# The modulation's matrix handed over transposed, its column sums taken by multiply-and-sum instructions on VectorE

## The chip, the cores and the metric

The kernel runs on one core of a Trainium2 chip. The metric is the time of one execution on the device, in microseconds (us): the median of three runs where several are shown. The engines that matter are TensorE (PE in the rows; PEld is its weight load), VectorE (DVE), ScalarE (ACT), GpSimd (POOL) and SyncE (SP, which issues nearly all DMAs). All data are 32-bit floats.

## The reference

Two transformer blocks are computed one after the other on 256 tokens of width 2048. The first is modulated by a condition vector `c`: six vectors of 2048 numbers (shift, scale and gate for the mixer, shift, scale and gate for the FFN) come from one large matrix-vector product, and everything in the block waits for some of them.

```python
c_act = jax.nn.silu(c)                       # 1 x 2048
mod = c_act @ w_ada[l] + b_ada[l]            # w_ada: 2048 x 12288
sh1, sc1, gt1, sh2, sc2, gt2 = jnp.split(mod, 6, axis=-1)
h = modulate(rms_norm(x, g_mix[l]), sh1, sc1)    # h * (1 + sc1) + sh1
z = h @ w_in[l]                              # projections, attentions, merge
x = x + gt1[:, None, :] * (merged @ w_out[l])
h = modulate(rms_norm(x, g_ffn[l]), sh2, sc2)
a = causal_dwconv(h @ w_gate[l], conv_w[l], conv_b[l])
x = x + gt2[:, None, :] * ((silu(a) * (h @ w_up[l])) @ w_down[l])
```

The second block has no modulation. `w_ada` is 2048 x 12288 numbers, 100.7 MB of the 581 MB that the kernel reads from HBM.

## The kernel before

Activations lie transposed: 128 features on the partitions, 256 tokens along a row. Weights stream through `rawp`, a pool of 6 buffers of 128 x 1024 numbers (10 at first, with `rawx`), each filled by one DMA from SP's queue. What is loaded, and in which order, is the list `items`: ("w", ...) is a piece of a weight matrix, ("ada", a, ...) a piece of `w_ada`, ("call", f) a function run at that point. `pump_loads` keeps up to `state["raws"]` items in flight beyond those already consumed.

A weight piece is consumed by `split`: ScalarE writes a rounded copy `wh` (line 296), VectorE the rest `wl = raw - wh` (line 303), and TensorE then does three products for each 128 x 128 tile (`mm_f`, lines 393 to 401, and `mm_t`, lines 412 to 414). `run` splits three pieces ahead of the one that TensorE multiplies (`AHEAD`). Everything is in program order on each engine; side work (attention, norms) is written as generators that `tick` moves on after a set amount of TensorE work.

**The modulation before.** `mod` is 128 x 96: column c holds features 128c to 128c+127 of the product. The 96 columns are taken in 28 groups (`ADA`): 12 groups of 2 or 3 columns for the first shift and scale, 16 groups of 4 columns for the rest. A piece of group `a` holds a few of the 16 row blocks k of `w_ada`, and `split` (lines 306 to 335) multiplies row block k, with the rows on the partitions, by the 128 numbers `cact[:, k]` and adds it into an accumulator `adaacc`. Two accumulators are filled side by side: VectorE does its share with one multiply-and-add each (line 330; the first with line 325), ScalarE scales the others (line 327) and GpSimd adds them (line 328). `ada_finish` lets GpSimd add both (line 366), and TensorE sums over the partitions by a product with a column of ones (line 370), from which VectorE writes `mod` (line 348). The first two groups, on which the first projection waits, are done in a hurry: of 16 row blocks VectorE takes ten and TensorE six (lines 321 and 355).

**Order around the change.** At the start SP loads `vec` (small vectors, `c` among them), `xT` and the first pieces. ScalarE computes `silu(c)` into `cact` (line 586, 128 x 16), then the squares of x (line 594); VectorE adds them up (lines 597, 598), TensorE sums over the partitions (line 601), `first_norm` turns the sums into `rb` (lines 607 to 613), `h_scale` multiplies x by it (line 626), `h_prep` applies the modulation (lines 635 to 648), and the first projection starts (line 399). The projections run in six stages of 2, 2, 3, 3, 3 and 3 row blocks (`KG`); during stage j the two groups that stage j + 1 needs are loaded and summed, mixed with the pieces of `w_in`. This lasts until about 415 us. The other 16 groups are spread over the gates, `w_o_sb`, `w_o_dsa`, `w_out` (until about 880 us) and the first FFN half, until 1040 us. `open_ffn` (line 1136), called before the first product with `w_out`, closes the pool `ab` of the first part and opens that of the FFN.

Of the kernel before, what the change touches and what calls it, by code (L numbers as in the profile page):

```python
# [28 lines left out]
FIRST_OWN = [k for k in range(16) if k % 8 not in (1, 4, 6)]  # L29
# [8 lines left out]
FW = (3, 3, 10)  # L38
# [16 lines left out]
VEC = [("c", 16), ("b_ada", 96), ("g_mix", 16), ("g_ffn", 16), ("g_final", 16), ("attn_norm", 16),  # L55
# [68 lines left out]
def kernel(ctx: ExitStack, tc: tile.TileContext, t):  # L124
# [30 lines left out]
    cact = const.tile([128, 16], F32, name="cact")  # L155
# [87 lines left out]
    def ada_items(a):  # L243
        return [("ada", a, k, n) for k, n in pieces(NK, 128 * ADA[a][1])]
# [7 lines left out]
    def load(idx):  # L252
# [11 lines left out]
        w = sum(g.width for g in it[1]) if it[0] == "w" else 128 * ADA[it[1]][1]  # L264
        r = raw_of[idx] = r[:, :n * w].rearrange("p (k w) -> p k w", w=w)
        if it[0] == "w":
            off = 0
            for width, src, c0, rmap in join([p for g in it[1] for p in g.parts]):
                nc.sync.dma_start(out=r[:, :, off:off + width], in_=rows(src, rmap(k0), n, c0, width))
                off += width  # L270
        else:
            nc.sync.dma_start(out=r, in_=rows(t["w_ada"], k0, n, 128 * ADA[it[1]][0], w))
# [9 lines left out]

    ada_acc = {}

    def split(idx, g, ks, off, stage):
# [20 lines left out]
        a = it[1]  # L306
        first = a in (0, NKG)
        if stage == 0 and k0 == 0:
            ada_acc[a] = P.get("ft", ab).tile([128, 2, 512], F32, name="adaacc", tag="adaacc", bufs=2)
            if first:  # L310
                ada_ps[a] = psm()
        for k in ks:
            side = k not in FIRST_OWN if first else k % 3 == 1 if a < 2 * NKG else k % 2 == 1
            if side != (stage == 0):
                continue
            own = FIRST_OWN.index(k) if first and not side else k // 2
            acc = ada_acc[a][:, own % 2 if first else int(side), :128 * ADA[a][1]]
            x, cs = r[:, k - it[2], :], cact[:, k:k + 1]
            if side and first:
                for j in range(ADA[a][1]):  # L320
                    nc.tensor.matmul(ada_ps[a][:, j:j + 1], x[:, 128 * j:128 * (j + 1)], cs,
                                     start=(k == 1 and j == 0), stop=False)
            elif own < (2 if first else 1):
                eng = nc.gpsimd if side else nc.vector
                eng.tensor_scalar(out=acc, in0=x, scalar1=cs, scalar2=None, op0=OP.mult)
            elif side:
                nc.scalar.activation(out=x, in_=x, func=AF.Copy, scale=cs)  # L327
                nc.gpsimd.tensor_tensor(out=acc, in0=x, in1=acc, op=OP.add)  # L328
            else:
                nc.vector.scalar_tensor_tensor(out=acc, in0=x, scalar=cs, in1=acc, op0=OP.mult, op1=OP.add)  # L330
        if stage == 1 and ks[-1] == NK - 1:
            if first:
                ada_first(a)
            else:
                fins.append(start(ada_finish(a)))

    ada_ps = {}
    ada_done = set()
    fins = []

    def need_ada(a, b):
        while not set(range(a, b)) <= ada_done:
            tick()

    def ada_put(a, ps, step):
        c, n = ADA[a]
        b = VOFF["b_ada"][0] + c
        nc.vector.tensor_add(out=mod[:, c:c + n], in0=ps[:, 0:step * n:step], in1=vec[:, b:b + n])
        ada_done.update(range(c, c + n))

    def ada_first(a):
        acc, ps, w = ada_acc.pop(a), ada_ps[a], 128 * ADA[a][1]
        nc.vector.tensor_add(out=acc[:, 0, :w], in0=acc[:, 0, :w], in1=acc[:, 1, :w])
        for j in range(ADA[a][1]):
            nc.tensor.matmul(ps[:, j:j + 1], acc[:, 0, 128 * j:128 * (j + 1)], ones[:, 0:1], start=False,
                             stop=(j == ADA[a][1] - 1))
        if a == 0:
            h_scale(0)
            ada_put(NKG, ada_ps[NKG], 1)
            ada_put(0, ps, 1)  # L360
# [1428 lines left out]
```

## Time and profile before

| | before |
|---|---|
| median of 3 runs | 2815.79 us (2815.03 to 2815.88) |
| the profiled execution, its own time | 2818.41 us |
| its span in the trace | 2816.6 us |
| TensorE busy | 2734.5 us (97%), 18364 instructions |
| VectorE busy | 2007.7 us (71%), 2804 instructions |
| ScalarE busy | 1424.9 us (51%), 2124 instructions |
| GpSimd busy | 841.1 us (30%), 710 instructions |
| DMA | 590.45 MB, mean 210 GB/s |

The page of the profile cuts the span into 40 slices and gives the busy share of each engine in tenths. TensorE reads 7899999899999999 for the first 16 slices and 9 in all that follow; VectorE 7999997979888986 first and 5 to 7 afterwards; GpSimd 3867752545754531 first and 0 to 3 afterwards. So the first 1030 us, in which the modulation runs, are the stretch where engines other than TensorE are full; after that TensorE is alone. A TensorE that reads as busy is not always multiplying at its peak, since the ends of its pipelined instructions are modelled: the idle time before an instruction, and what ended it, say more than the busy share.

### The profile page before, as it was taken

Reading aid. Unit: us, or ns where it says so; the run is one execution under the profiler, and the core shown is the slowest. Engines: PE = TensorE matmul, PEld = TensorE weight load, DVE = VectorE, ACT = ScalarE, POOL = GpSimd, SP = SyncE. Lnnn points to the kernel's source line nnn. Section 1 sums busy time; section 2 is a strip of 40 time slices with the busy share of each in tenths; the row PEclk is TensorE's granted clock in tenths of the full one; section 3 lists DMA queues with packets and bytes.
Section 4 is the critical chain, followed back from the end, with each engine's and each line's share of the span. In section 5 each row is a group of like instructions: output and inputs, shape, how many; then the busy total and the mean of one; then the engine's idle time right before and its main releaser. Section 6 shows DMA issues by size and latency. Waiting matters only on the chain.

```text
span 2816.6 us, 47791 instructions
## 1 busy us (share of the span) xinstructions
PE 2734.5 (97%) x18364; PEld 2496.7 (89%) x18364; DVE 2007.7 (71%) x2804; ACT 1424.9 (51%) x2124; POOL 841.1 (30%) x710
## 2 busy tenths in 40 slices
PE   7899999899999999999999999999999999999999
PEld 7788887788988999989999888989998888888888
DVE  7999997979888986655666765676776665556654
ACT  5555564555556554434454544555554544344443
POOL 3867752545754531000110310211222220012210
PEclk9999999999999999999999999999999999999999
DMA  9777777878887876566666575544566565566654
GB/s 316 250 249 256 241 219 203 268 242 280 291 276 233 287 260 183 184 188 186 180 180 191 183 229 172 163 123 144 186 188 187 180 189 193 187 187 187 187 195 142
DMA packets 334944, 590.45 MB, mean 210 GB/s; under 512 B 21234, under 2 KB 85594, under 8 KB 334716
## 3 DMA queue, kind: packets, MB, share of 16 engines
q1 hardware_dynamic: 331236, 583.61, 65.7%
q10 hardware_dynamic: 3480, 3.79, 0.7%
q8 instruction: 144, 2.36, 0.3%
q14 instruction: 84, 0.69, 0.1%
HBM read 581.49 MB, written 5.78 MB: 209 GB/s over the span
## 4 chain that ended last, share of the span: by engine, by line
PE 76%; DVE 10%; DMA 5%; issue 4%; POOL 3%; ACT 2%; SPq 0%; DVEq 0%; ACTq 0%; POOLq 0%
PE pg L397 25%; PE pg L396 13%; PE pg L399 9%; PE pg L400 9%; PE pg L401 9%; DVE wl L303 4%; DVE adaacc L330 3%; PE pg L393 2%; DMA raw<-in_w_in 2%; PE pm L728 1%; PE pg L412 1%; ACT wh L296 1%; PE pg L414 1%; PE pg L413 1%; DMA raw<-in_w_out 1%
## 5 line engine op out<-in xcount | busy, mean ns | idle before, releaser
L303 DVE TENSOR_TENSOR wl<-raw,wh 128x1024 fp32r<-128x1024 f32 (+1 forms) x921 | 1192.1, 1306 | 658.3 <-ACT wh L296 656.1
L296 ACT ACTIVATE wh<-raw 128x1024 fp32r<-128x1024 f32 (+2 forms) x922 | 934.2, 1026 | 883.2 <-PE pg L397 497.6
L397 PE MATMUL pg<-ring,wh 128*128 128x512 f32 x3384 | 1203.9, 396 | 0.0
L396 PE MATMUL pg<-ring,wl 128*128 128x256 f32 x3384 | 957.9, 283 | 7.6 <-DVE wl L303 7.6
L399 PE MATMUL pg<-ring,wh 128*128 128x256 f32 (+1 forms) x2828 | 813.7, 288 | 9.8 <-DVE ring L1093 3.6
L401 PE MATMUL pg<-ring,wl 128*128 128x256 f32 (+1 forms) x2828 | 799.9, 283 | 13.9 <-DVE wl L303 13.8
L400 PE MATMUL pg<-ring,wh 128*128 128x256 f32 (+1 forms) x2828 | 803.7, 284 | 0.0
L397 PEld LDWEIGHTS pg<-ring,wh 128*128 128x128 f32 x3384 | 638.2, 189 | 141.4
L396 PEld LDWEIGHTS pg<-ring,wl 128*128 128x128 f32 x3384 | 638.4, 189 | 23.6 <-DVE wl L303 9.5
L401 PEld LDWEIGHTS pg<-ring,wl 128*128 128x128 f32 x2828 | 541.4, 191 | 17.8 <-DVE wl L303 17.8
L399 PEld LDWEIGHTS pg<-ring,wh 128*128 128x128 f32 x2828 | 538.2, 190 | 19.7 <-issue 7.6
L400 PEld LDWEIGHTS pg<-ring,wh 128*128 128x128 f32 x2828 | 539.5, 191 | 3.6 <-issue 2.2
L531 POOL TENSOR_TENSOR ring<-gy,ring 128x256 fp32r<-128x256 f32 x88 | 107.1, 1230 | 661.9 <-ACT ring L529 661.9
L328 POOL TENSOR_TENSOR adaacc<-raw,adaacc 128x512 f32<-128x512 f32 (+2 forms) x152 | 230.6, 1517 | 247.4 <-ACT raw L327 197.4
L330 DVE SCALAR_TENSOR_TENSOR adaacc<-raw,cact,adaacc 128x512 f32<-128x512 f32 (+2 forms) x228 | 234.2, 1031 | 3.6 <-DMA raw<-in_w_ada 2.0
L1268 POOL TENSOR_TENSOR gy<-ga,rb 128x256 f32<-128x256 f32 x44 | 53.6, 1228 | 331.1 <-ACT ga L203 331.1
L516 POOL TENSOR_TENSOR ring<-pt,ring 128x256 f32<-128x256 f32 x95 | 109.7, 1167 | 50.5 <-ACT pt L515 50.3
L327 ACT ACTIVATE raw<-raw,cact 128x512 f32<-128x512 f32 (+2 forms) x152 | 103.1, 681 | 23.3 <-DMA raw<-in_w_ada 16.9
L1163 POOL TENSOR_TENSOR ssq<-ssq,sq 128x256 f32<-128x256 f32 x60 | 63.8, 1075 | 145.3 <-ACT sq L1161 144.0
L1406 POOL TENSOR_TENSOR hm<-hm,hsq 128x512 f32<-128x512 f32 (+1 forms) x15 | 18.4, 1224 | 286.3 <-ACT hsq L203 286.3
L393 PE MATMUL pg<-ring,wh 128*128 128x512 f32 x200 | 81.9, 410 | 7.0 <-DVE ring L1169 3.6
L412 PE MATMUL pg<-wh,ring 128*128 128x512 f32 (+3 forms) x236 | 84.2, 357 | 0.0
(300 smaller groups left out, 2665.1 us busy)
## 6 DMA issues: line engine op xcount, KB each, us to landing
raw<-in_w_in SPq DMA_DIRECT2D x240, 512.0 KB, 4.6
raw<-in_w_gate SPq DMA_DIRECT2D x176, 512.0 KB, 4.2
raw<-in_w_up SPq DMA_DIRECT2D x176, 512.0 KB, 4.4
raw<-in_w_down SPq DMA_DIRECT2D x176, 512.0 KB, 4.2
raw<-in_w_ada SPq DMA_DIRECT2D x144, 512.0 KB, 5.4
raw<-in_w_out SPq DMA_DIRECT2D x64, 512.0 KB, 4.6
raw<-in_w_ada SPq DMA_DIRECT2D x64, 384.0 KB, 4.1
raw<-in_w_o_sb SPq DMA_DIRECT2D x16, 512.0 KB, 5.1
```

What stands on the lines that cost most here:

```text
L296: nc.scalar.activation(out=hi, in_=src, func=AF.Copy)
L303: nc.vector.tensor_sub(out=lo, in0=src, in1=hi.bitcast(F32))
L328: nc.gpsimd.tensor_tensor(out=acc, in0=x, in1=acc, op=OP.add)
L330: nc.vector.scalar_tensor_tensor(out=acc, in0=x, scalar=cs, in1=acc, op0=OP.mult, op1=OP.add)
L393: nc.tensor.matmul(g.ps[f], hi[:, fs], both, start=True, stop=False)
L396: nc.tensor.matmul(ps, lo[:, fs], xh, start=False, stop=False)
L397: nc.tensor.matmul(g.ps[f], hi[:, fs], both, start=False, stop=stop)
L399: nc.tensor.matmul(ps, hi[:, fs], xh, start=start, stop=False)
L400: nc.tensor.matmul(ps, hi[:, fs], xl, start=False, stop=False)
L401: nc.tensor.matmul(ps, lo[:, fs], xh, start=False, stop=stop)
L412: nc.tensor.matmul(ps, xh[:, bs], hi, start=start, stop=False)
L516: nc.gpsimd.tensor_tensor(out=y, in0=x, in1=y, op=OP.add)
```

## The change

`w_ada` is handed over transposed (`w_adaT`, 12288 x 2048, prepared outside the kernel as the other inputs are), and an item is now one half of a column block: 128 outputs on the partitions, 1024 of the 2048 inputs along the row. One VectorE instruction multiplies the piece by the same half of `silu(c)`, which lies in every partition (`cb`, 128 x 2048), and sums along the row into `mod[:, c]`. The first half starts from `b_ada`, the second from what the first left. ScalarE, GpSimd and TensorE no longer take part.

To have `silu(c)` in every partition, `c` is loaded as one row, TensorE multiplies it by a row of ones (four products of 128 x 512), and ScalarE writes the silu of each into `cb`. One row of it goes to HBM (`cdram`), since the pool with `cb` is closed by `open_ffn`; there a second `cb` is opened and filled from `cdram` by a DMA from ScalarE's queue.

```diff
     def ada_items(a):
-        return [("ada", a, k, n) for k, n in pieces(NK, 128 * ADA[a][1])]
+        return [("ada", a, i, 1) for i in range(2 * ADA[a][1])]
...
+        if it[0] == "ada":
+            raw_of[idx] = r
+            c, half = ADA[it[1]][0] + it[2] // 2, it[2] % 2
+            nc.sync.dma_start(out=r, in_=t["w_adaT"][128 * c:128 * c + 128, RAW * half:RAW * half + RAW])
+            return
...
-            if side and first:
-                for j in range(ADA[a][1]):
-                    nc.tensor.matmul(ada_ps[a][:, j:j + 1], x[:, 128 * j:128 * (j + 1)], cs,
-                                     start=(k == 1 and j == 0), stop=False)
-            elif own < (2 if first else 1):
-                eng = nc.gpsimd if side else nc.vector
-                eng.tensor_scalar(out=acc, in0=x, scalar1=cs, scalar2=None, op0=OP.mult)
-            elif side:
-                nc.scalar.activation(out=x, in_=x, func=AF.Copy, scale=cs)
-                nc.gpsimd.tensor_tensor(out=acc, in0=x, in1=acc, op=OP.add)
-            else:
-                nc.vector.scalar_tensor_tensor(out=acc, in0=x, scalar=cs, in1=acc, op0=OP.mult, op1=OP.add)
...
+        if stage == 0:
+            return
+
+        c, half = ADA[it[1]][0] + it[2] // 2, it[2] % 2
+        below = mod[:, c:c + 1] if half else V["b_ada"][:, c:c + 1]
+        nc.vector.tensor_tensor_reduce(out=r, in0=r, in1=P["cb"][:, RAW * half:RAW * half + RAW], scale=1.0,
+                                       scalar=below, op0=OP.mult, op1=OP.add, accum_out=mod[:, c:c + 1])
+        if half:
+            ada_done.add(c)
...
-    def ada_finish(a):
-        acc, w = ada_acc.pop(a), 128 * ADA[a][1]
-        s = acc[:, 1, :w]
-        yield
-        nc.gpsimd.tensor_tensor(out=s, in0=acc[:, 0, :w], in1=s, op=OP.add)
-        yield from wait(FW[a // NKG if a < 2 * NKG else 2])
-        ps = psm()
-        for j in range(ADA[a][1]):
-            nc.tensor.matmul(ps[:, j:j + 1], s[:, 128 * j:128 * (j + 1)], ones[:, 0:1], start=True, stop=True)
-        ada_put(a, ps, 1)
...
+    P["cb"] = ab.tile([128, D], F32, name="cb")
+    nc.sync.dma_start(out=P["cb"][0:1, :], in_=t["c"])
...
-    lut(out=cact, in_=V["c"], func=AF.Silu)
+    for u in range(4):
+        ps = psm()
+        nc.tensor.matmul(ps, ones[0:1, :], P["cb"][0:1, 512 * u:512 * u + 512], start=True, stop=True)
+        lut(out=P["cb"][:, 512 * u:512 * u + 512], in_=ps, func=AF.Silu)
+    cdram = dram.tile([1, D], F32, name="cdram")
+    nc.scalar.dma_start(out=cdram, in_=P["cb"][0:1, :])
...
-    a0, a1 = ada_items(NKG), ada_items(0)
+    a0 = ada_items(NKG) + ada_items(0)
     items.extend(a0[:2])
     call_item(first_norm)
-    items.extend(a0[2:] + a1)
+    items.extend(a0[2:-2])
+    call_item(lambda: h_scale(0))
+    items.extend(a0[-2:])
     call_item(first_h)
...
+            if first:
+                P["cb"] = P["ft"].tile([128, D], F32, name="cb", bufs=1)
+                nc.scalar.dma_start(out=P["cb"], in_=bass.AP(tensor=cdram.tensor, offset=cdram.offset,
+                                                             ap=[[0, 128], [1, D]]))
```

The programs of both kernels show where this puts the instructions. First ScalarE from the start of the program to `first_norm`; `mm` and `r` are the norm's scratch tiles. Before:

```order
L203 ACT_TABLE_LOAD
L203 ACTIVATE cact<-vec 128x16
L594 ACTIVATE ring<-ring 128x1024 x4
L607 ACTIVATE mm<-pm,epsc 128x256
L197 ACT_TABLE_LOAD
```

Now:

```order
L200 ACT_TABLE_LOAD
L200 ACTIVATE cb<-pm 128x512 x4
L538 DMA cdram<-cb 1x2048
L546 ACTIVATE ring<-ring 128x1024 x4
L559 ACTIVATE mm<-pm,epsc 128x256
L194 ACT_TABLE_LOAD
```

The four squares of x (line 594, now 546) stand behind four silus instead of one short one, each of which waits for a product of TensorE, and behind the issue of a DMA.

Second, VectorE in the third projection stage, the stretch that the sum below turns on. Lines 303 and 300 are the same instruction before and now; 518, 520, 463 and 465 take projections out of PSUM. A row with ISA is the multiply-and-sum (128x1024) or the short read of its sum (128x1). Before:

```order
L330 SCALAR_TENSOR_TENSOR adaacc<-raw,cact,adaacc 128x384
L303 TENSOR_TENSOR wl<-raw,wh 128x1024
L330 SCALAR_TENSOR_TENSOR adaacc<-raw,cact,adaacc 128x384 x2
L303 TENSOR_TENSOR wl<-raw,wh 128x512
L520 SCALAR_TENSOR_TENSOR ring<-pm,ring 128x256 x2
L303 TENSOR_TENSOR wl<-raw,wh 128x512
L330 SCALAR_TENSOR_TENSOR adaacc<-raw,cact,adaacc 128x384
L303 TENSOR_TENSOR wl<-raw,wh 128x1024
```

Now:

```order
L308 ISA raw,mod<-raw,cb,vec 128x1024
L308 ISA mod 128x1
L300 TENSOR_TENSOR wl<-raw,wh 128x1024
L308 ISA raw,mod<-raw,cb,mod 128x1024
L308 ISA mod 128x1
L300 TENSOR_TENSOR wl<-raw,wh 128x512
L465 SCALAR_TENSOR_TENSOR ring<-pm,ring 128x256 x2
L300 TENSOR_TENSOR wl<-raw,wh 128x512
L300 TENSOR_TENSOR wl<-raw,wh 128x1024
```

One instruction of 1024 stands where one or two of 384 stood, and every one of them is VectorE's.

Third, VectorE where `open_ffn` is called; the row `gain` is the last instruction of that function on VectorE. Before:

```order
L348 TENSOR_TENSOR mod<-pm,vec 128x4
L1145 SCALAR_TENSOR_TENSOR gain<-mod,vec 128x16
L303 TENSOR_TENSOR wl<-raw,wh 128x1024
L325 TENSOR_SCALAR adaacc<-raw,cact 128x512
L303 TENSOR_TENSOR wl<-raw,wh 128x1024
L330 SCALAR_TENSOR_TENSOR adaacc<-raw,cact,adaacc 128x512
```

Now:

```order
L1098 SCALAR_TENSOR_TENSOR gain<-mod,vec 128x16
L300 TENSOR_TENSOR wl<-raw,wh 128x1024
L308 ISA raw,mod<-raw,cb,vec 128x1024
L308 ISA mod 128x1
L300 TENSOR_TENSOR wl<-raw,wh 128x1024
L308 ISA raw,mod<-raw,cb,mod 128x1024
```

The first multiply-and-sum after `gain` reads the second `cb`, whose DMA is issued at that place; it stands two instructions behind.

## Rows read from the trace of the kernel before

**Rows 1.** Busy time by stretch: length, then each engine (instructions), clock, DMA.

```profile
core 0: us, PE busy (x) PEld busy (x) DVE busy (x) ACT busy (x) POOL busy (x), PEclk, DMA share, GB/s
0.00:31.00 31.00, 15.80 (x65) 15.00 (x65) 15.52 (x38) 10.12 (x14) 6.19 (x10) 1.00 1.00 326
31.00:400.00 369.00, 342.14 (x2395) 315.88 (x2396) 347.11 (x470) 211.17 (x388) 259.30 (x215) 0.98 0.80 254
400.00:1030.00 630.00, 598.26 (x4017) 544.20 (x4016) 539.13 (x730) 352.64 (x517) 325.95 (x246) 0.98 0.80 259
1030.00:2816.00 1786.00, 1778.30 (x11892) 1621.62 (x11890) 1105.90 (x1569) 850.99 (x1207) 249.62 (x241) 1.00 0.59 181
```

**Rows 2.** The chain of waits in 70 to 400 us, by line.

```profile
by line: DVE wl L303 16.8%; issue 15.5%; DVE adaacc L330 13.1%; DMA raw<-in_w_in 5.6%; PE pg L401 4.7%; PE pg L399 4.3%; PE pg L400 4.1%; DVE ring L518 2.4%; POOL ring L516 2.3%; POOL adaacc L366 2.1%; ACT wh L296 2.0%; DVE ring L520 1.9%; 
```

**Rows 3.** VectorE's largest groups in 70 to 400 us: busy us, mean ns.

```profile
L303 DVE TENSOR_TENSOR wl<-raw,wh 128x1024 fp32r<-128x1024 f32 x70 | 105.4, 1506 | 8.6 <-ACT wh L296 8.6
L330 DVE SCALAR_TENSOR_TENSOR adaacc<-raw,cact,adaacc 128x384 f32<-128x384 f32 x80 | 82.7, 1033 | 1.1
L303 DVE TENSOR_TENSOR wl<-raw,wh 128x512 fp32r<-128x512 f32 x56 | 51.6, 922 | 0.4 <-ACT wh L296 0.2
```

**Rows 4.** The tile adaacc alone, by stretch: PE, PEld, DVE, POOL, clock, DMA.

```profile
31.00:400.00 369.00, 8.15 (x64) 8.30 (x64) 115.78 (x122) 99.14 (x72) 0.98 0.80 254
400.00:1030.00 630.00, 13.57 (x112) 14.29 (x112) 130.07 (x116) 226.57 (x131) 0.98 0.80 259
```

**Rows 5.** Softmax's sum-as-you-go instruction (line 869) and its read, whole run.

```profile
L869 DVE CUSTOM_DVE_ANT_0 t<-pm,t 128x256 f32<-128x256 f32 x32 | 13.4, 418 | 0.8 <-POOL t L901 0.4 <-POOL t L1652 0.4
...
L869 DVE CUSTOM_DVE_ANT_0 t<-pm,t 128x128 f32<-128x128 f32 x32 | 9.0, 282 | 1.3 <-PE pm L891 0.4 <-POOL t L900 0.4 <-POOL t L1651 0.4
...
L869 DVE DVE_READ_ACCUMULATOR2_ANT st<- 128x1 f32 x64 | 5.2, 81 | 0.0
```

**Rows 6.** Lines 303 and 330 in 400 to 600 us: shortest/median/longest ns.

```profile
L303 DVE TENSOR_TENSOR wl<-raw,wh x51: 1208/1220/2343, 399.5 to 598.1; 128x1024 fp32r<-128x1024 f32 x51
...
L330 DVE SCALAR_TENSOR_TENSOR adaacc<-raw,cact,adaacc x27: 736/745/1775, 415.1 to 596.3; 128x512 f32<-128x512 f32 x27
```

**Rows 7.** TensorE's waits in 31 to 1030 us: total, times, longest.

```profile
PE pm L370 <- POOL adaacc L366: 5.7, 4, 2.2
```

**Rows 8.** Timeline of the start: start us, us, instruction, idle time before.

```profile
3.22 0.22 ACT L203 ACTIVATE cact<-vec 128x16 f32<-128x16 f32 x1 [1.20 <-DMA vec<-in_vec]
...
10.36 1.06 ACT L594 ACTIVATE ring<-ring 128x1024 f32<-128x1024 f32 x1 [0.44 <-DMA ring<-in_xT]
...
13.98 3.78 PE L601 MATMUL pm<-ring,ones 128*128 128x256 f32 x8 [13.98 <-DVE ring L598]
...
22.76 0.77 POOL L613 TENSOR_TENSOR rb<-r,mm 128x256 f32<-128x256 f32 x1
...
29.62 0.15 DVE L635 SCALAR_TENSOR_TENSOR gain<-mod,vec 128x2 f32<-128x2 f32 x1
...
30.72 0.58 PE L399 MATMUL pg<-ring,wh 128*128 128x256 f32 x1 [1.22 <-ACT ring L644]
```

**Rows 9.** A ScalarE function over 512 numbers from PSUM.

```profile
L1402 ACT ACTIVATE hm<-pm,epsc 128x512 f32<-128x512 f32 (+1 forms) x15 | 9.8, 654 | 11.9 <-DVE ring L1413 7.4 <-PE pm L1398 2.0 <-DVE lf L1620 1.4
```

**Rows 10.** VectorE's timeline where open_ffn is called.

```profile
775.08 0.63 DVE L1145 SCALAR_TENSOR_TENSOR gain<-mod,vec 128x16 f32<-128x16 f32 x1
775.63 1.21 DVE L303 TENSOR_TENSOR wl<-raw,wh 128x1024 fp32r<-128x1024 f32 x1
776.77 0.96 DVE L325 TENSOR_SCALAR adaacc<-raw,cact 128x512 f32<-128x512 f32 x1
```

**Rows 11.** DMA issues: count, KB each, us from issue to landing.

```profile
raw<-in_w_down SPq DMA_DIRECT2D x176, 512.0 KB, 4.2
raw<-in_w_ada SPq DMA_DIRECT2D x144, 512.0 KB, 5.4
...
ydram<-ring SPq DMA_DIRECT2D x2, 1024.0 KB, 6.2
```

More of the change, by code (lines that the diff above doesn't have):

```diff
@@ L28 @@
 TOPK = 3
-FIRST_OWN = [k for k in range(16) if k % 8 not in (1, 4, 6)]
 LATE_SMALL = (3, 2)
@@ L154 @@
     invp = const.tile([128, 1], F32, name="invp")
-    cact = const.tile([128, 16], F32, name="cact")
     mod = const.tile([128, 96], F32, name="mod")
@@ L262, in load @@
             return
+        if it[0] == "ada":
[3 more added lines that the diff above has]
+            return
         k0, n = it[2], it[3]
-        w = sum(g.width for g in it[1]) if it[0] == "w" else 128 * ADA[it[1]][1]
+        w = sum(g.width for g in it[1])
         r = raw_of[idx] = r[:, :n * w].rearrange("p (k w) -> p k w", w=w)
[L266 to L270, printed above, removed]
-        else:
-            nc.sync.dma_start(out=r, in_=rows(t["w_ada"], k0, n, 128 * ADA[it[1]][0], w))
+        off = 0
+        for width, src, c0, rmap in join([p for g in it[1] for p in g.parts]):
+            nc.sync.dma_start(out=r[:, :, off:off + width], in_=rows(src, rmap(k0), n, c0, width))
+            off += width
     def join(parts):
@@ L305, in split @@
             return
[L306 to L318, printed above, removed]
-            if side and first:
-                for j in range(ADA[a][1]):
-                    nc.tensor.matmul(ada_ps[a][:, j:j + 1], x[:, 128 * j:128 * (j + 1)], cs,
-                                     start=(k == 1 and j == 0), stop=False)
-            elif own < (2 if first else 1):
-                eng = nc.gpsimd if side else nc.vector
-                eng.tensor_scalar(out=acc, in0=x, scalar1=cs, scalar2=None, op0=OP.mult)
-            elif side:
-                nc.scalar.activation(out=x, in_=x, func=AF.Copy, scale=cs)
-                nc.gpsimd.tensor_tensor(out=acc, in0=x, in1=acc, op=OP.add)
-            else:
-                nc.vector.scalar_tensor_tensor(out=acc, in0=x, scalar=cs, in1=acc, op0=OP.mult, op1=OP.add)
@@ L331, in split @@
[L331 to L337, printed above, removed]
+        if stage == 0:
[4 more added lines that the diff above has]
+                                       scalar=below, op0=OP.mult, op1=OP.add, accum_out=mod[:, c:c + 1])
@@ L338 @@
+        if half:
+            ada_done.add(c)
     ada_done = set()
-    fins = []
     def need_ada(a, b):
[L342 to L353, printed above, removed]
-        for j in range(ADA[a][1]):
[L355 to L360, printed above, removed]
@@ L362, in ada_finish @@
-    def ada_finish(a):
-        acc, w = ada_acc.pop(a), 128 * ADA[a][1]
-        s = acc[:, 1, :w]
-        yield
-        nc.gpsimd.tensor_tensor(out=s, in0=acc[:, 0, :w], in1=s, op=OP.add)
-        yield from wait(FW[a // NKG if a < 2 * NKG else 2])
-        ps = psm()
-        for j in range(ADA[a][1]):
-            nc.tensor.matmul(ps[:, j:j + 1], s[:, 128 * j:128 * (j + 1)], ones[:, 0:1], start=True, stop=True)
-        ada_put(a, ps, 1)
+        assert set(range(a, b)) <= ada_done, (a, b, ada_done)
@@ L1763 @@
          "slc_k": "slc_k_norm_2", "win_k": "win_k_norm_2", "pos_k": "cmp_pos_k_2", "pos_v": "cmp_pos_v_2"}
-_INS = {"w_ada": "w_ada", "w_in": "w_in", "w_o_sb": "w_o_sb", "w_o_dsa": "w_o_dsa", "w_out": "w_out",
+_INS = {"w_in": "w_in", "w_o_sb": "w_o_sb", "w_o_dsa": "w_o_dsa", "w_out": "w_out",
         "rel_bias": "rel_bias", "w_gate": "w_gate", "w_up": "w_up", "w_down": "w_down", "w_in_2": "w_in_2",
@@ L1776 @@
               "con": shape_constants(),
+              "c": np.ascontiguousarray(a["c"].reshape(1, D)),
+              "w_adaT": np.ascontiguousarray(a["w_ada"][0].T),
               "xT": np.ascontiguousarray(a["x"][0].T)}
```

7 lines of the change are left out of this document (2 added, 5 removed).

## The prediction

> **What bounds the kernel now.** I read the table by stretch first [rows 1]: it tells which engine is full where. From 1030 us to the end TensorE is busy 1778.3 of 1786 us, and nothing of the modulation runs there; that part I leave as it is. In the projections, 31 to 400 us, TensorE idles for 26.9 us and VectorE is busy 347.1 of 369 us (94%). The chain of waits in that stretch [rows 2] agrees: its largest shares are VectorE's, 16.8% the remainders of line 303 and 13.1% the multiply-and-adds of line 330. So VectorE sets the pace there. From 400 to 1030 us it is mixed: TensorE idles 31.7 us, VectorE is busy 86%. The next view is VectorE's groups [rows 3]: both large ones are much longer on the mean than they need be. A remainder of 1024 numbers takes 1506 ns there, but 1208 ns at its shortest [rows 6]; the reader should see that this goes with GpSimd, busy 259 of 369 us. Then what the change removes, by the tile `adaacc` alone [rows 4], and last the only instruction of the new kind that the trace has [rows 5].
>
> **The change, part by part.** Times below are of the profiled execution, 2818.4 us, whose span is 2816.6 us; the 1.8 us around it stay. It is 2.6 us above the median of the runs, which I take off at the end. A difference of 0.2% (5.6 us) is about what a measurement here can tell from no change.
>
> *Price of one multiply-and-sum.* Line 869 takes 282 ns for 128 numbers and 418 ns for 256 [rows 5]: 136 ns for 128 more, 1.06 ns each. For 1024 that is 418 + 768 x 1.06 = 1234 ns, plus 81 ns for the read of the sum. Consecutive instructions of VectorE overlap by some 0.08 us (the gain begins at 775.08, takes 0.63, and the next begins at 775.63 [rows 10]), so one costs 1.24 us of the engine. Line 869 has one input in PSUM, the new one both in SBUF; the remainder of line 303, with both in SBUF, takes 1.21 us for 1024 [rows 6], so I take 1.24. The bounds are 1.21 and 2.34 us, the shortest and the longest remainder of that size [rows 6]; the upper end is a rival below.
>
> [...] The trace shows that two inputs in SBUF alone do not slow an instruction: line 330, without a running sum out, takes 736 ns for 512 numbers [rows 6], the rate of line 869. [...]
>
> *The projections, 31 to 400 us.* Leaves VectorE: 115.8 us in 122 instructions [rows 4]. Comes: 68 multiply-and-sums (56 for the 28 columns that stages 1 to 5 need, and 12 early ones of the later groups, which is what those 12 of the 122 instructions with 512 numbers stand for), 68 x 1.24 = 84 us. Relief: GpSimd loses 99.1 of its 259.3 us [rows 1, 4], a factor of 0.62. The remainders are over their shortest by 70 x 0.30 + 56 x 0.25 = 35 us (1506 against 1208; 922 against 0.67, half of 1208 and of the 120 ns that 1.06 ns a number leaves over) [rows 3, 6], 28% on some 122 us; 0.62 of that saves 13 us and puts 17%, 14 us, on the new instructions. Sum: 347 - 116 + 84 + 14 - 13 = 316 us, 31 less. TensorE also loses the 8.2 us of line 370 [rows 4]. With VectorE no longer full, TensorE's products are next; it cannot go below 342.1 - 8.2 = 334 us. I take 344 us, **25 less**. Bounds: 8 less (only line 370, with DMA or ScalarE late instead) and 35 less (all idle time gone as well).
>
> *400 to 1030 us.* TensorE loses 13.6 us of line 370 [rows 4] and its waits for GpSimd's addition, 5.7 us in both stretches [rows 7], of which I count 4. VectorE loses 130.1 and gets 116 x 1.24 = 144 us: 553 of 630 before any relief from GpSimd, which loses 226.6 of 326 us [rows 1, 4]. It stays under TensorE's 598. **18 less**; bounds 5 less and 32 less.
>
> *The start.* Now the squares of x wait for four silus, and these for four products of 512 columns. Four products of 256 take 3.78 us [rows 8], so these take 7.6, from about 3 us, when `vec` had landed [rows 8], to 10.6; the last silu over 512 numbers ends 0.65 us later [rows 9], and the DMA's issue adds some 0.4. The first square starts at 11.7 and four of 1.06 end at 15.9, where they ended at 11.4 [rows 8]. All behind them shifts by 4.5 us: `rb` is ready at 28 instead of 23.5. From there the order is `h_scale` (0.7), two multiply-and-sums (2.5), gain: 31.4 instead of 29.6 [rows 8]. The first projection, 1.1 us behind, starts near 32.5: **2 more**. Bounds: 3 less (squares not late, as TensorE's sums of lines 321 and 355 are gone) and 5 more.
>
> *The second `cb`.* VectorE reaches the first ada instruction 1.7 us behind the gain [rows 10]. The DMA of 1 MB is issued about when the gain runs, and one of that size takes 6.2 us to land [rows 11]; VectorE stands some 5 us, and the remainders behind it with it. TensorE is up to three pieces behind, so I count **3 more**; bounds 0 and 9.
>
> *Costed at nothing.* ScalarE's scaling (line 327) goes, but ScalarE is busy 57% there [rows 1]. SP issues 192 loads of 512 KB, the same bytes as before. A piece is now 4 KB per partition at a pitch of 8 KB; `w_down`, at that pitch, lands in 4.2 us against 5.4 for `w_ada` [rows 11], so I see no loss. If DMA were slower after all, the first stretch would lose its gain (second rival). Buffers come free when VectorE is through, where GpSimd was later; what a faster VectorE triggers is denser loading, from 254 to some 272 GB/s at a DMA share of 0.80 [rows 1].
>
> Sum: -25 - 18 + 2 + 3 = -38. 2818.4 - 38 - 2.6 = **2778 us**.
>
> **The rivals.**
> 1. *Half rate, slower.* The multiply-and-sum takes twice the time per number, 1.09 us more each. VectorE then has 316 + 74 = 390 us of work in the projections and 553 + 126 = 679, less some 30 of relief, behind them. At its 94% that is 415 and 690 us: 46 and 60 longer. With start and `cb` 2815.8 + 46 + 60 + 5 = 2927 us. It decides from 1.24 + 31 / 68 = 1.7 us per instruction on: there the projections are as slow as before. [...] Against it: rows 5 and 6, each at 1.06 ns a number. Chance 0.13.
> 2. *DMA or buffers take VectorE's place.* The projections load at a DMA share of 0.80, and at 1.00 in the first 31 us [rows 1]; the pieces of `w_in` then land late and only line 370's 8 us are won: -8 - 18 + 5 = -21, 2795 us. Chance 0.2.
> 3. *The matmul slots were free.* TensorE's removed products only fill time in which it waits for remainders, and VectorE's relief stays small since line 516 keeps GpSimd busy: about 5 won, 5 lost, 2816 us. Chance 0.1, half of it over and half under that.
>
> That the change doesn't do what it says can be left out: the rows of the program show the new instructions alone.
>
> **How the numbers follow.** The forecast, 2778 us, has 0.57, with a range of its own from 2748 (all upper gains but the start's) to 2795. Rival 2 is faster too. Faster by over 0.2%: 0.57 + 0.2 - 0.02 for a poor case of it = 0.75. Within 0.2%: 0.07, most of rival 3. Slower: 0.18, rival 1 and the tails of 3 and of the start. The range runs from 2748 to 2822, which leaves out rival 1 and a little on the low side.
>
> **What would show it.** In the profile after: the multiply-and-sum of 1024 near 1.23 us (right) or 2.3 (rival 1); VectorE below 90% and TensorE idle under 15 us in the 345 us behind the start; remainders under 1.4 us there; the first product of line 399's successor near 32.5 us; a wait of VectorE for the DMA of `cb` of some 5 us near 740 us. If TensorE's or ScalarE's waits for raw pieces grow by over 15 us in the projections, it is rival 2. I am wrong if VectorE is still above 94% there.

## The result, and the profile after

The changed kernel takes 2766.2 us (median of 4 runs, 2764.53 to 2767.92) beside 2815.84 us before (2815.03 to 2817.10): a ratio of 0.9825, 95% interval 0.9813 to 0.9837, 49.6 us faster. The forecast of 2778 us lies 12 us above it; the measured time is inside its range (2748 to 2822). The profiled execution took 2767.92 us, its span is 2765.9.

The table by stretch of the changed kernel, cut as in [rows 1]:

```profile
core 0: us, PE busy (x) PEld busy (x) DVE busy (x) ACT busy (x) POOL busy (x), PEclk, DMA share, GB/s
0.00:31.00 31.00, 10.91 (x16) 5.01 (x16) 14.94 (x23) 11.10 (x14) 7.03 (x10) 1.00 0.94 347
31.00:400.00 369.00, 342.52 (x2411) 316.21 (x2412) 338.82 (x499) 198.27 (x354) 170.96 (x147) 0.99 0.79 258
400.00:1030.00 630.00, 612.42 (x4240) 561.69 (x4239) 532.77 (x859) 303.66 (x434) 109.98 (x119) 1.00 0.82 273
```

GpSimd fell from 326 to 110 us behind 400 us, ScalarE from 353 to 304. VectorE is still busy 92% of the projections, against 94%. But equal stretches of the clock no longer hold equal work. So I cut by milestones: the first product of the projections (30.7 us before, 34.9 after), the first gate product (416.1, 403.5), VectorE's first evacuation of an FFN gate (895.2, 849.3) and the end. The two stages between them, first before, then after:

```profile
31.00:416.00 385.00, 358.14 (x2504) 330.65 (x2505) 360.34 (x495) 220.99 (x405) 262.46 (x219) 0.98 0.79 251
416.00:895.00 479.00, 448.36 (x2802) 396.40 (x2802) 400.64 (x546) 258.65 (x381) 252.75 (x188) 0.98 0.80 255
```

```profile
35.00:403.50 368.50, 345.96 (x2440) 319.65 (x2441) 338.56 (x498) 199.36 (x356) 170.46 (x146) 0.99 0.79 258
403.50:849.00 445.50, 427.92 (x2704) 377.19 (x2703) 383.68 (x626) 208.09 (x302) 91.23 (x87) 1.00 0.83 276
```

The start lost 4 us, the projections gained 17, the next stage 33, the rest 5. In that next stage TensorE is busy 20 us less and idle 13 us less (30.6 to 17.6). Before, some 27 of its idle 30.6 us ended with an instruction of VectorE and 2.8 with one of GpSimd; after, some 17 of 17.6 with VectorE's. Of the 20, some 12 are its 98 fewer products, at 121 ns each by [rows 4] (13.57 us for 112). The other 8 go with the granted clock, on the mean 0.98 before and 1.00 after: 2% of some 430 us, an estimate.

The multiply-and-sum, by its line (shortest/median/longest ns):

```profile
L308 DVE DVE_READ_ACCUMULATOR2_ANT mod<- x192: 74/80/88, 18.4 to 975.3; 128x1 f32 x192
L308 DVE CUSTOM_DVE_ANT_0 raw<-raw,cb,vec x96: 1268/1277/2314, 17.2 to 969.6; 128x1024 f32<-128x1024 f32 x96
L308 DVE CUSTOM_DVE_ANT_0 raw<-raw,cb,mod x96: 1265/1279/2064, 18.5 to 974.1; 128x1024 f32<-128x1024 f32 x96
```

VectorE's remainders of 1024 numbers in 400 to 1000 us, before and after:

```profile
L303 DVE TENSOR_TENSOR wl<-raw,wh 128x1024 fp32r<-128x1024 f32 x175 | 257.3, 1484 | 64.5 <-ACT wh L296 64.1
```

```profile
L300 DVE TENSOR_TENSOR wl<-raw,wh 128x1024 fp32r<-128x1024 f32 x189 | 244.0, 1303 | 60.9 <-ACT wh L293 60.7
```

Behind the projections the same subtraction became 181 ns shorter on the mean. In the projections it did not (31 to 400 us; 1480 ns for 83 of them before):

```profile
L300 DVE TENSOR_TENSOR wl<-raw,wh 128x1024 fp32r<-128x1024 f32 x87 | 125.7, 1447 | 7.6 <-ACT wh L293 7.0 <-DMA raw<-in_w_adaT 0.5
```

And VectorE still leads the chain of waits there (31 to 380 us):

```profile
by line: DVE wl L300 23.0%; DVE raw L308 18.9%; issue 14.4%; DMA raw<-in_w_in 5.5%; PE pg L346 3.9%; PE pg L344 3.5%; PE pg L345 3.4%; DVE ring L463 3.4%; PE pm L346 2.9%; PE pm L344 2.6%; PE pm L345 2.6%; DMA raw<-in_w_adaT 2.5%; DVE ring 
```

### The profile page after: what moved, and what is told of

Same layout as the page of the kernel before. It is cut to its first block, busy times and chain, and to the rows that moved or that the text cites. A ratio compares the mean times of both kernels' runs of the same rounds, so it can differ in the third digit from the quotient of the medians.

```text
span 2765.9 us, 46663 instructions
## 1 busy us (share of the span) xinstructions
PE 2692.9 (97%) x18132; PEld 2453.5 (89%) x18132; DVE 1959.5 (71%) x2900; ACT 1339.5 (48%) x1975; POOL 530.6 (19%) x506
## 4 chain that ended last, share of the span: by engine, by line
PE 80%; DVE 10%; DMA 4%; issue 3%; POOL 1%; ACT 1%; SPq 0%; ACTq 0%; DVEq 0%; POOLq 0%
PE pg L342 26%; PE pg L341 13%; PE pg L344 10%; PE pg L345 10%; PE pg L346 10%; DVE wl L300 4%; DVE raw L308 4%; DMA raw<-in_w_in 2%; PE pg L338 1%; PE pm L680 1%; PE pg L357 1%; DMA raw<-in_w_out 1%; PE pg L358 1%; PE pg L359 1%; PE pg L339 1%
## 5 line engine op out<-in xcount | busy, mean ns | idle before, releaser
L300 DVE TENSOR_TENSOR wl<-raw,wh 128x1024 fp32r<-128x1024 f32 (+1 forms) x921 | 1154.3, 1265 | 648.5 <-ACT wh L293 642.8
L308 DVE CUSTOM_DVE_ANT_0 raw<-raw,cb,mod 128x1024 f32<-128x1024 f32 x96 | 134.4, 1400 | 1.5 <-DMA raw<-in_w_adaT 1.3
L308 DVE CUSTOM_DVE_ANT_0 raw<-raw,cb,vec 128x1024 f32<-128x1024 f32 x96 | 128.9, 1343 | 1.9 <-DMA cb<-cdram 1.8
L346 PE MATMUL pm<-ring,wl 128*128 128x256 f32 x260 | 75.1, 289 | 4.8 <-DVE wl L300 4.8
L358 PE MATMUL pg<-wl,ring 128*128 128x512 f32 (+3 forms) x236 | 79.0, 335 | 0.0
```

The lines of the kernel that those rows point to most:

```text
L300: nc.vector.tensor_sub(out=lo, in0=src, in1=hi.bitcast(F32))
L308: nc.vector.tensor_tensor_reduce(out=r, in0=r, in1=P["cb"][:, RAW * half:RAW * half + RAW], scale=1.0, scalar=below, op0=OP.mult, op1=OP.a ...
L346: nc.tensor.matmul(ps, lo[:, fs], xh, start=False, stop=stop)
L358: nc.tensor.matmul(ps, xh[:, bs], lo, start=False, stop=False)
```

## The experiments

**Which engine's relief was it?** Three things left other engines than VectorE: GpSimd's additions, TensorE's closing products, ScalarE's scalings. Each was put back alone into the changed kernel, on scratch tiles that nobody waits for. `load_back` is called in `split` for each ada piece, at the place where ScalarE would round a weight piece. The names of the scratch tiles are shortened.

```diff
+    def load_back(a, i):
+        n, w = ADA[a][1], 128 * ADA[a][1]
+        for _ in range(1 if n == 4 else 1 + (i == 0) if n == 2 else int(i < 5)):
+            nc.gpsimd.tensor_tensor(out=dp[:, :w], in0=ones_bc, in1=dp[:, :w], op=OP.add)
+        if i == 2 * n - 1:
+            start(end_back(n))
```

This is GpSimd's; `ones_bc` stands for `ones` repeated n times along the row, and `end_back` does one addition more. For TensorE `end_back` alone remains, with n products `matmul(ps[:, j:j + 1], dp[:, 128 * j:128 * (j + 1)], ones[:, 0:1])` and a VectorE copy of their sums; for ScalarE the line in the loop is an `activation` with `AF.Copy` and a factor.

*GpSimd alone (e1_pool).*

> The changed kernel with only GpSimd's old load put back: one 128x(128n) addition on a scratch tile for each product that GpSimd used to add (168 of them beside the two first column groups), and one more at the end of each group; nobody waits for them. Theory A (most of the gain after the start is GpSimd: its queue no longer delays the attention chains, and its additions no longer slow VectorE's two-input instructions): 20 to 30 us of the 49.6 come back, 2786 to 2796 us, with VectorE's 128x1024 remainders and multiply-and-sums slower by 0.05 to 0.1 us each. Theory B (the gain is TensorE's removed products): at most 5 us, 2764 to 2771 us. Theory C (ScalarE's removed scalings): the same as B here.

Measured: 2906.54 us (ratio to before 1.0327, 1.0309 to 1.0344), 140 us over the changed kernel. Theory A has the sign and the place, and is five times too small. The dummies took 352 us of GpSimd, hardly more than the 326 us of [rows 4]. The stages of this kernel (to its first gate product at 453.1 us, to its first FFN gate at 970.4), and VectorE's large groups in 400 to 1000 us:

```profile
35.00:453.00 418.00, 359.59 (x2440) 329.47 (x2441) 382.65 (x494) 200.71 (x356) 292.35 (x221) 0.96 0.72 228
453.00:970.00 517.00, 457.12 (x2708) 398.23 (x2707) 465.28 (x632) 208.36 (x303) 278.01 (x191) 0.94 0.74 239
```

```profile
L312 DVE TENSOR_TENSOR wl<-raw,wh 128x1024 fp32r<-128x1024 f32 x156 | 240.4, 1553 | 42.6 <-ACT wh L305 42.4
L322 DVE CUSTOM_DVE_ANT_0 raw<-raw,cb,vec 128x1024 f32<-128x1024 f32 x50 | 79.2, 1584 | 0.1
```

The remainders are 0.25 us longer than in the changed kernel (1303 ns), not 0.05 to 0.1. For the same work VectorE is busy 44 us longer in the first stage and 82 in the second. VectorE's instructions that take one of their inputs from PSUM did not get longer (31 to 400 us; 412 ns in the changed kernel too):

```profile
L477 DVE TENSOR_TENSOR ring<-pg,ring 128x256 f32<-128x256 f32 x28 | 10.9, 412 | 6.8 <-PE pg L360 6.8
```

TensorE waits on VectorE, busy 88% of the second stage, and its granted clock there is 0.94 on the mean, 1.00 in the changed kernel.

*TensorE alone (e2_pe).*

> The changed kernel with only TensorE's old closing products put back: n products of one column per group (184 in the kernel before took 22.7 us) from a scratch tile that is always ready, and one small VectorE copy. Theory B: each late product costs its own duration, 64 of them in the projections are partly hidden by VectorE, so 16 to 23 us come back, 2782 to 2789 us. Theory A: TensorE has gaps to hold them, at most 6 us, 2764 to 2772 us. Theory C: as A.

Measured: 2780.24 us (0.9878, 0.9863 to 0.9893), 14.0 us back. The trace has the dummies as

```profile
L293 PE MATMUL pm<-ones,dp 128*128 128x1 f32 x184 | 22.2, 239 | 2.6 <-POOL dp L1124 2.0 <-ACT pt L476 0.7
```

so some two thirds of their time reach the end. The first gate product comes 2.6 us later than in the changed kernel (406.1 us), the first FFN gate 8.7 us later (858.0): in the projections most of it is hidden by VectorE, behind them little. Theory B holds in kind, for 14 of 50 us, a little under its 16 to 23. Up to 2.0 us of this is TensorE's wait for the scratch tile to be cleared (`dp L1124` in the row), which the old products did not have.

*ScalarE alone (e3_act).*

> The changed kernel with only ScalarE's old scalings put back: one 128x(128n) copy with a factor, from constants to a scratch tile, for each scaling that the kernel before ran (152 there, 103 us in all). Theory C (ScalarE's queue delayed the evacuations and roundings): 10 to 25 us come back, 2776 to 2791 us. Theories A and B: ScalarE is busy half of the time and hides them, at most 5 us, 2764 to 2771 us.

Measured: 2769.37 us (0.9837, 0.9823 to 0.9852), 3.2 us back, and the two intervals overlap: ScalarE hid nearly all of its scalings. Theory C falls.

*All three (e4_all).*

> The three loads together. If the loads on the three engines are the whole of the gain and VectorE's exchanged work is worth nothing by itself, all but the start's own change comes back: 2810 to 2822 us (54 us of gain after a start that lost 4.2). If a part of the gain is that VectorE's own instructions became fewer or that buffers come free earlier, less comes back: 2780 to 2800 us. Theory A: the sum is within 8 us of e1 alone; theory B: within 8 us of e2 alone.

Measured: 2919.55 us (1.0374, 1.0358 to 1.0389), 153 us back, beside 140 + 14 + 3 = 157 for the three alone. They add up. No case was right: I had not considered that the loads together cost more in the changed kernel than the whole change won.

**GpSimd's queue, or its reads beside VectorE's (e5_memset)?**

```diff
-            nc.gpsimd.tensor_tensor(out=dp[:, :w], in0=ones_bc, in1=dp[:, :w], op=OP.add)
+            [nc.gpsimd.memset(dp[:, :w], 0.0) for _ in range(3)]
```

> As e1_pool, but each addition on GpSimd is three memsets of the same scratch tile, which take about as long (540 ns each for 128x512) and read nothing; only what GpSimd's instructions read is changed. If the 140 us of e1_pool came from GpSimd's queue (the additions of attention and convolution behind the dummies), nearly the same comes back: 2880 to 2910 us. If they came from GpSimd's two-input additions slowing VectorE's two-input instructions (multiply-and-sums 1.37 to 1.65 us, remainders 1.28 to 1.48 us in e1_pool), then VectorE's durations stay as in the changed kernel and the time too: 2764 to 2780 us.

Measured: 2768.19 us (0.9833, 0.9818 to 0.9848), 2 us over the changed kernel, and GpSimd is as full as in the kernel before:

```profile
31.00:400.00 369.00, 347.19 (x2466) 322.88 (x2467) 341.05 (x505) 203.45 (x361) 270.28 (x378) 0.99 0.79 262
400.00:1030.00 630.00, 607.59 (x4185) 556.82 (x4184) 529.93 (x850) 299.06 (x427) 305.51 (x497) 0.99 0.81 271
```

The queue theory falls: 300 us of GpSimd instructions that read nothing cost 2 us, within the scatter, and VectorE's remainders in 400 to 1000 us stay at 1300 ns (1303 in the changed kernel). GpSimd's additions of e1, which read two tiles, cost 140 us, and beside them VectorE's remainders (1303 to 1553 ns on the mean) and multiply-and-sums (1336 to 1571 ns, both in 400 to 1000 us), which have two inputs in SBUF, became longer; those with an input in PSUM did not (412 ns in both). One collision of the changed kernel, VectorE's timeline and then GpSimd's (start us, duration):

```profile
256.67 1.86 DVE L308 CUSTOM_DVE_ANT_0 raw<-raw,cb,vec 128x1024 f32<-128x1024 f32 x1
...
260.32 1.28 DVE L308 CUSTOM_DVE_ANT_0 raw<-raw,cb,mod 128x1024 f32<-128x1024 f32 x1
...
261.53 1.75 DVE L300 TENSOR_TENSOR wl<-raw,wh 128x1024 fp32r<-128x1024 f32 x1
```

```profile
256.70 0.74 POOL L461 TENSOR_TENSOR ringv<-pt,ringv 128x256 f32<-128x256 f32 x1 [1.34 <-ACT pt L460]
...
260.53 1.67 POOL L461 TENSOR_TENSOR ring<-pt,ring 128x256 f32<-128x256 f32 x1 [0.79 <-ACT pt L460]
```

At 256.7 us VectorE's instruction is 0.6 us longer and GpSimd's runs undisturbed; at 260.5 us VectorE's is undisturbed and GpSimd's takes 1.67 instead of 0.74 us. Either may be the one that loses.

**GpSimd's relief alone, on the kernel before (e6_before_no_pool).**

```diff
+            elif side and not first:
+                nc.scalar.activation(out=x, in_=x, func=AF.Copy, scale=cs)
...
-        s = acc[:, 1, :w]
+        s = acc[:, 0, :w]
         yield
-        nc.gpsimd.tensor_tensor(out=s, in0=acc[:, 0, :w], in1=s, op=OP.add)
```

> The kernel before with GpSimd's part of the modulation left out (its 152 additions and first products, and the 26 closing additions; the even blocks' sum alone goes to TensorE, so the modulation lacks the products that ScalarE scales). ScalarE's scalings and TensorE's closing products stay. If VectorE was slowed in the kernel before as in e1_pool, its late remainders go from 1484 to about 1300 ns and the time falls by 30 to 60 us, below the changed kernel: 2755 to 2785 us. If the kernel before was bound by TensorE after the projections whatever GpSimd did, at most 10 us: 2805 to 2815 us.

Measured: 2744.35 us beside 2815.22 (0.9748, 0.9734 to 0.9763), 71 us faster, 22 us below the changed kernel and 11 us below the forecast. Its stages, to a first gate product at 380.3 us and a first FFN gate at 820.4:

```profile
31.00:380.00 349.00, 344.82 (x2502) 324.62 (x2502) 316.75 (x494) 225.59 (x417) 146.94 (x146) 1.00 0.84 277
380.00:820.00 440.00, 433.10 (x2788) 386.44 (x2787) 333.57 (x547) 265.18 (x392) 80.45 (x87) 1.00 0.84 278
```

VectorE's late remainders (400 to 1000 us) are at the changed kernel's 1303 ns:

```profile
L303 DVE TENSOR_TENSOR wl<-raw,wh 128x1024 fp32r<-128x1024 f32 x191 | 246.7, 1301 | 114.6 <-ACT wh L296 114.2
```

TensorE is busy 99% of the projections. So GpSimd's additions held the kernel before, and taking them away is worth more than the whole change. For the same work VectorE is busy 44 us less in the first stage and 67 us less in the second. But GpSimd's additions and first products were also the last to read some of the load buffers. SP waited for them before its next load, in the kernel before (31 to 1030 us; total, times, longest), and does not here:

```profile
SPq L269 <- POOL adaacc L328: 30.9, 16, 6.0
SPq L272 <- POOL adaacc L328: 21.9, 9, 4.3
SPq L272 <- POOL adaacc L325: 16.5, 9, 3.8
SPq L269 <- POOL adaacc L325: 11.3, 7, 2.5
```

In the projections that hardly matters: ScalarE, which rounds first, waited there 0.5 us in all for weight pieces. In the second stage it waited 63 us for them in the kernel before, 33 us here and 88 us in the changed kernel. So a part of these 71 us may be buffers that come free earlier, and no run parts it from VectorE's relief. What the changed kernel gained in that stage is not a shorter wait for pieces.

**What VectorE's added work costs (e10_half).**

```diff
+        if half and it[1] not in (0, NKG):
+            ada_done.add(c)
+            return
```

> The changed kernel with the second multiply-and-sum of every column left out but for the four columns of the start (so half of the modulation's products are missing); the transfers stay. It takes some 125 us of work from VectorE and nothing else. If VectorE's added work is what holds the changed kernel back (GpSimd's relief alone made the kernel before 71 us faster, the whole change only 50): 2725 to 2745 us, with TensorE over 97% busy from 31 us on. If transfers and buffers hold it: 2755 to 2766 us.

Measured: 2730.76 us (0.9694, 0.9677 to 0.9710), 35 us below the changed kernel. The first gate product comes at 376.0 us, with TensorE busy

```profile
31.00:376.00 345.00, 336.19 (x2441) 316.74 (x2442) 293.21 (x437) 199.79 (x357) 164.69 (x147) 0.99 0.83 279
```

97% (the first 4 us of this stretch are start). Transfers kept up at 279 GB/s; VectorE holds the changed kernel. A piece that is not multiplied also gives its buffer back sooner, which this run doesn't part from VectorE's time; but VectorE is what the buffers wait for: in the changed kernel SP waits 636 us in all between 31 and 1030 us for VectorE's remainders and multiply-and-sums before its next loads.

**VectorE's load moved within the kernel (e8_more0).** `MORE` 12 to 0, `RL` (0.75, 0.6) to (0.9, 0.6).

> The changed kernel with twelve multiply-and-sums moved out of the last projection stage into the stages behind it (no constant of them is dropped; the rate at which the later stages take them is raised for one of the two output stages from 0.75 to 0.9). If VectorE bounds the projections and TensorE the stages behind them: 12 x 1.36 us of VectorE work leave the projections, the first gate product comes 10 to 16 us earlier (403 to about 390 us) and the end 6 to 16 us earlier, 2750 to 2760 us. If transfers and buffers bound the projections, or if VectorE bounds the stages behind as well: no change, 2763 to 2770 us.

Measured: 2773.69 us (0.9852, 0.9837 to 0.9866), 7.5 us slower: a miss. The first gate product came 4.7 us earlier (398.8), less than half of the forecast, and that lead was lost between the first sum of `w_o_dsa` and the first sum of `w_out`, where VectorE is now busy 55.0 of 63 us:

```profile
691.00:754.00 63.00, 58.50 (x413) 55.34 (x412) 54.98 (x65) 27.92 (x37) 39.34 (x32) 0.95 0.93 326
```

In the changed kernel that stage takes 57.7 us with TensorE full. TensorE's idle 4.5 us there are one wait, for a sum of `w_o_dsa` (L1059) that stands on VectorE behind five multiply-and-sums in a row and two remainders (720.5 to 730.9 us); four of the five took 1.65 to 1.76 us, beside GpSimd. The changed kernel has one multiply-and-sum at a time there. ScalarE's waits for pieces of `w_out` are the same in both (9.6 and 9.5 us), so it isn't the transfers. A stage whose mean shows room on VectorE had none at that point. How much of the loss is the raised rate and how much the later columns was not tried apart.

**The start (e7_start).** `h_scale(0)` behind `a0[2:]` instead of `a0[2:-2]`, and `FIRSTS = 0`.

> The changed kernel with the first scaling of x put behind all eight multiply-and-sums of the start (it stood before the last two, so VectorE waited 2.7 us for rb and did both afterwards), and with the first remainder on VectorE instead of GpSimd, so that nothing on GpSimd runs beside the scaling (2.81 us there, 0.69 us in the kernel before). If the start's lost time is this order: the first product of the projections comes 4 to 6 us earlier (34.9 to about 30 us) and the kernel takes 2760 to 2763 us. If the end does not follow the start because VectorE, which bounds the projections, has the same work: 2764 to 2767 us.

Measured: 2766.00 us (0.9828, 0.9812 to 0.9845): no difference that can be measured. The first product did come earlier, at 32.1 us, but not at 30: `rb`, the end of a chain on GpSimd, was late, since two of its last three instructions now ran beside multiply-and-sums (0.72, 0.41 and 0.72 us for the three in the changed kernel):

```profile
25.58 1.58 POOL L563 TENSOR_TENSOR mm<-mm,r 128x256 f32<-128x256 f32 x1
27.25 1.26 POOL L564 TENSOR_SCALAR mm<-mm 128x256 f32<-128x256 f32 x1
28.60 0.72 POOL L565 TENSOR_TENSOR rb<-r,mm 128x256 f32<-128x256 f32 x1
```

The profiled run keeps 2.8 us at the first gate product (400.7), within the scatter of the times.

**The collisions that are left (e9_put_vector).** In the projections GpSimd still does 140 additions.

```diff
-            if alt():
-                x = ab.tile([128, T], F32, name="pt", tag="pt", bufs=2)
-                nc.scalar.activation(out=x, in_=ps[:, o:o + T], func=AF.Copy, scale=...)
-                nc.gpsimd.tensor_tensor(out=y, in0=x, in1=y, op=OP.add)
-            elif scale is None:
+            if scale is None:
                 nc.vector.tensor_tensor(out=y, in0=ps[:, o:o + T], in1=y, op=OP.add)
```

> The changed kernel with the 140 additions of partial sums that GpSimd still does in the projections (157 us of GpSimd there, after a copy on ScalarE) done by VectorE straight from PSUM, at 0.41 us each as for those that VectorE does already. If a GpSimd addition costs VectorE about what it takes while a multiply-and-sum or a remainder runs beside it (0.38 us of VectorE for each us of GpSimd by e1_pool, so 60 us), this is an even exchange for VectorE's 58 us: 2758 to 2774 us, with the remainders of the projections at about 1250 ns instead of 1447. If those additions hardly collide, VectorE, which bounds the projections, pays: 2790 to 2820 us.

Measured: 2757.14 us (0.9791, 0.9776 to 0.9805), 9 us faster than the changed kernel and 1 us below the forecast's even exchange, with the first gate product at 394.2 us. The projections, and the remainders in 31 to 400 us:

```profile
35.00:394.00 359.00, 340.73 (x2438) 318.16 (x2439) 342.77 (x643) 156.39 (x217) 6.18 (x5) 0.98 0.80 266
```

```profile
L300 DVE TENSOR_TENSOR wl<-raw,wh 128x1024 fp32r<-128x1024 f32 x89 | 108.6, 1223 | 6.4 <-ACT wh L293 6.4
```

VectorE took over some 58 us of additions and its busy time in the projections grew by 4 (338.6 to 342.8). The rest it got back from collisions: 54 us for the 161 us that these additions took on GpSimd, some 41 of them in the remainders (1447 to 1223 ns on the mean for 1024 numbers, 912 to 691 for 512) and the multiply-and-sums (1436 to 1315 ns). The gain in time is idle time of VectorE, 30 us in the changed kernel and 16 here; 8.1 us of those 30 had ended with ScalarE's copies `pt`, which are gone:

```profile
L463 DVE TENSOR_TENSOR ringv<-pg,ringv 128x256 f32<-128x256 f32 x24 | 9.4, 414 | 8.1 <-ACT pt L460 8.1
```

**Together (e11_best, e12_best_late).** e9 with the start of e7 and the chain of `rb` on VectorE; then `hilo_gen`'s remainders and the additions of the gated outputs on VectorE too.

> e9_put_vector with the start of e7_start, and with the four small instructions that make rb moved from GpSimd, where e7_start showed them slowed to 5.4 us beside multiply-and-sums, to VectorE behind the eight multiply-and-sums (some 1.5 us). If the start is what its order makes it: first product of the projections at about 31 us (34.9 in the changed kernel, 32.1 in e7_start), first gate product at about 390 us (394.2 in e9_put_vector), and 2751 to 2755 us. If VectorE swallows the start as it did in e7_start: 2755 to 2759 us.

> e11_best with two more kinds of GpSimd additions on VectorE: the 128x256 remainders of attention and the modulation gate (32 of them before 1030 us at 1.2 to 1.6 us on GpSimd, and 68 behind) and the 16 additions of the gated outputs (0.92 us each). GpSimd between 400 and 1030 us falls from 113 to about 60 us, VectorE takes some 16 us more there and its remainders lose what collisions they have. If collisions with GpSimd still hold VectorE behind the projections: 3 to 8 us faster than e11_best. If TensorE (97% busy there) holds that part: within 2 us of e11_best. If VectorE's queue delays the attention chains: slower by 2 to 6 us.

Measured: 2755.67 us (0.9791, 0.9778 to 0.9804) and 2755.70 us (0.9790, 0.9777 to 0.9804). Both are the fastest complete kernels here, 10.5 us below the changed one; neither differs from e9 by more than the scatter. In e11 the first product came at 33.4 us, not 31: seven scalings of GpSimd, 10.5 us in all from 29.25 us on, now start beside VectorE's last steps, and two subtractions take 2.90 us (0.76 in the changed kernel). Two scalings of VectorE (L594, one large input and two numbers per partition) take 2.59 us there, 0.73 in the changed kernel: not only instructions with two large inputs are slowed. VectorE swallows the start again; the first gate product comes at 392.4 us. In e12 GpSimd fell to 54 us behind the projections and nothing moved: there TensorE, 98% busy, leaves nothing to win that way.

## Why the prediction was right, and where it was not

- **Price of one multiply-and-sum: right.** 1277 ns at the median, one start to the next 1.21 to 1.33 us in the run of six at the start, against 1.24. The doubled time of the first rival, 1.09 us more each, no run shows as the price: with two 32-bit inputs in SBUF and a running sum the instruction takes, at the median, 1.25 ns per number with all overhead.
- **Start: +4 instead of +2.** The products took 7.2 us and `rb` came at 27.5, as worked out (7.6 and 28). Missed was what GpSimd does at that moment: its one remainder and its scaling ran beside `h_scale` and the next multiply-and-sum.

```profile
27.57 2.81 DVE L578 TENSOR_TENSOR ring<-ring,rb 128x512 f32<-128x512 f32 x1 [2.71 <-POOL rb L565]
30.30 2.28 DVE L308 CUSTOM_DVE_ANT_0 raw<-raw,cb,vec 128x1024 f32<-128x1024 f32 x1
```

```profile
27.49 2.34 POOL L298 TENSOR_TENSOR wl<-raw,wh 128x1024 fp32r<-128x1024 f32 x1
29.79 1.71 POOL L578 TENSOR_TENSOR ring<-ring,rb 128x512 f32<-128x512 f32 x1
```

- **Projections: -17 instead of -25.** The failed step is the relief by GpSimd's busy time, the factor of 0.62. The remainders were to fall under 1.4 us and stayed at 1447 ns, VectorE was to fall to 316 us, below 90%, and stayed at 339 us, 92%, and TensorE, which was to idle under 15 us, idles for 22.5. The 140 additions that GpSimd keeps there still collide: without them (e9) the remainder is at 1223 ns.
- **Behind the projections: -38 instead of -18 + 3.** The products of TensorE were near their size here: 13.6 us counted, 14.0 us for all 184 in e2, of which some 11 behind the projections; in the projections 8 were counted and 2.6 came. The failed step is "553 of 630 before any relief": I gave VectorE's relief no time there, since its mean load stayed under TensorE's. But GpSimd's additions did hold that stage in the kernel before: without them (e6) it takes 440 us instead of 479, with remainders 183 ns shorter on the mean. The changed kernel's are 181 ns shorter, its ScalarE waits no less for weight pieces, and some 27 of TensorE's 30.6 idle us had ended with VectorE; so what it won there beyond TensorE's products I put down to VectorE's relief. How much of e6's 39 us is buffers is open.
- **The second `cb`: +3 was too much.** VectorE waited 1.8 us for it, not 5, since the DMA was issued 4.5 us ahead of the gain and not with it (it took 8.0 us to land, not 6.2), and the stage in which it stands (first sum of `w_o_dsa` to that of `w_out`) went from 61.6 to 57.7 us.
- **Rivals.** DMA did not take VectorE's place (258 GB/s at a share of 0.79, and 279 when VectorE had less to do; ScalarE waited under 1 us for weight pieces in the projections, before and after; a piece of `w_adaT` lands in 5.5 us at the median, one of `w_ada` in 5.4). The matmul slots were not free (14 us).
- **The range.** With the start at its +2, the upper gains give 2751 us, not 2748; it changes nothing.

So the total is as near as it is by luck: two errors, 10 us too hopeful up to 400 us and 23 us too cautious behind, cancel in part. In one account: GpSimd's additions -71 (e6), TensorE's products -14, ScalarE's scalings -3, the start +4 make -84 us. Measured are -50; the 34 that are missing are what is left for VectorE's exchange of work. That last number is a difference, not a measurement: a microsecond of GpSimd does not cost the same in both kernels, 71 us for 326 in the kernel before and 140 us for 352 in the changed one. Why it costs more in the changed one, no run shows.

## What to carry to other kernels

Before work is moved off GpSimd, look at what VectorE runs beside it. Here the mean of a VectorE group against its shortest instruction showed the collisions (remainders behind the projections: 1484 ns on the mean, 1208 at the shortest, and 1301 on the mean without GpSimd's part of the modulation), and they were worth more than the moved work itself (71 us in e6, buffers included, and 50 for the whole change). Such a relief counted where VectorE's work was waited for, also in a stage where its mean load was below that of the leading engine: in the second stage of the kernel before VectorE was busy 84% and TensorE 94%, and e6 made that stage 39 us shorter, buffers included. An addition of two SBUF tiles on GpSimd was no free help with VectorE 92% busy: 140 of them done on VectorE straight from PSUM (e9) were 58 us of its work and made it busy for 4 us more, and took a copy and a queue out of the way.

## What the runs showed of the hardware

- 352 us of GpSimd additions, which read two tiles, cost 140 us (e1); 300 us of GpSimd memsets in their places, which read none, cost 2 us (e5).
- The collisions go both ways: three of the four small GpSimd instructions that end in `rb` took two to three times as long beside multiply-and-sums (e7: 1.50, 1.58 and 1.26 us; 0.73, 0.79 and 0.45 in the kernel before), and `h_scale` took 2.81 instead of 0.69 us beside GpSimd's remainder.
- A multiply-and-sum over 1024 32-bit numbers with both inputs in SBUF costs 1.28 us and 80 ns for the read, overlapped to some 1.28 us apiece; a plain subtraction, nearly all of that size, takes 1226 ns at the median (behind 1100 us).
